# Seven-product up projection of a conv FFN: bank-freeing sum ahead of the gate's products, persistent convolution tiles, small copies on ACT, one weight and the last norms on DVE

## The chip, the cores and the metric

The kernel runs on one core of one Trainium2 chip. The core has five engines that run side by side: TensorE (PE, matrix products), VectorE (DVE, elementwise), ScalarE (ACT, elementwise functions and copies), GpSimd (POOL, elementwise) and SyncE (SP, which issues loads). PE writes into the banks of PSUM; the other operands lie in SBUF. Each engine works through its own list in order, and waits by semaphores for the others. The metric is the device time of one execution in microseconds (us).

## The reference

A decoder block on x of 1024 tokens by 1024 channels, in float32. Two token mixers are merged by gates, and a convolutional FFN follows; its part is the one that the change touches:

```
u = h @ w_up                                   # 1024 -> 2 x 2816
u = sum(up[:, i:i + T] * conv_w[i] for i in range(3)) + conv_b
gate, val = split(u, 2)
out = (gelu(gate, approximate=True) * val) @ w_down
```

The result is normalised by its root mean square over the channels, scaled, and added to the residual h.

## The kernel before

Channels lie on the 128 partitions and tokens on the free axis, in two halves of 512. A float32 product is made of three matmuls on parts: each operand is cast to a high part (`w_hi`, `b_hi`) and the rest is taken as a low part (`w_lo`, `b_lo`), and lines L225, L226 and L227 are high x high, high x low and low x high. ACT makes the casts. The subtraction of a weight's low part is made by POOL or DVE: `load_w` (L219) chooses by a count, or takes the engine named in `eng`.

The up projection has 22 pairs of channel tiles (a gate tile, index b = 0, and a value tile, b = 1). The first NSTD = 3 pairs are made by `up_std`, plainly, once per half (`hf`). Each copies a product from PSUM into `ub`, a tile with two extra columns ahead of the 512 for the three-step convolution. For the second half these two columns come from `carry`, which the first half filled: copies of 128 x 2 on POOL (L1100, L1103). The convolution `conv` is one ACT step (L1066) and two DVE steps (L1067, L1069). `gate` applies gelu on ACT (L1075 or L1223), multiplies gate and value on DVE (L1076) and stores the product to `f_d` in HBM by a DMA that ACT issues (L1077).

The other 19 pairs use seven products in place of eight (a two-by-two block scheme over halves of the channels and the halves of the tokens). Its weights are sums of weight halves, made on DVE: `w_sa` at L1175 and L1176, two more in place at L1178 and L1179. ACT casts them (L1171) and POOL subtracts (L1172), except one half that DVE does. POOL's subtraction of `w_sa` must be through before DVE may write the next `w_sa` into the same buffer two tiles later. The inputs are T1 to T4, sums of `hn2`'s halves made on DVE from `n_d`, loaded back from HBM (L1129 to L1135), with low parts at L962. The products go to the banks `ps_x`, `ps_z`, `ps_t` and `ps_y`: 84 matmuls per pair. ACT copies `ps_x` to s1 (L1197) and `ps_z` to s5 (L1205); DVE's sum L1207 reads `ps_t`, and from then on PE may run the second group into it; L1209, L1215 and L1217 are the other sums that read PSUM, and L1213 on POOL adds s1 and s5 in SBUF. For the first NEAR = 4 pairs the `ps_x` part was computed earlier and comes from HBM.

The second half of a pair's gate work (convolution of the value tile, products, stores) is the function `rest`, which the next pair's code calls, right behind the copy of s1. The order of instructions on each engine comes from a scheduler that takes the code's order and moves what has a priority (`WPRIO` for weights, `GPRIO` for `rest`).

The down projection and its norm end the kernel. `post_norm` is called for 512 tokens and then twice for 256: there each of eight output tiles is multiplied by the broadcast root `rm_b` (L931) and added to the residual (L932), shared between DVE, which reads `rm_b` from PSUM, and POOL, which reads a copy that ACT makes (L920).

## Time and profile before

| what | value |
|---|---|
| median of 3 timed runs | 1880.75 us (1874.88 to 1882.73) |
| profiled execution, its own time | 1882.48 us |
| its span, first to last instruction | 1880.7 us |
| mean granted TensorE clock | 0.978 of full speed |
| PE busy | 1788.1 us (95% of the span) |
| DVE busy | 1177.7 us (63%) |
| ACT busy | 648.9 us (35%) |
| POOL busy | 687.7 us (37%) |

Busy PE time contains overlap of pipelined matmuls, so the number of matmuls that start in a stretch tells more than its busy share. The seven-product loop fills the stretch from about 1250 to 1611 us, its steady part the stretch from 1345 to 1565; the down projection and the last norm follow to the end.

### The profile page before, as it was taken

The page shows a single profiled execution, that of the slowest core. Times are in us where ns is not written, and L with a number is a line of the kernel's source. Part 1 is how long each engine was busy: PE and PEld are TensorE (multiplying, and loading weights), DVE is VectorE, ACT ScalarE, POOL GpSimd, SP SyncE. Part 2 cuts the span into 40 slices and gives each one's busy share as a digit, 9 for nine tenths or more (in the row PEclk, how much of TensorE's full clock was granted, in tenths as well). Part 3 has the DMA queues.
Part 4 walks back from the last instruction along what each step waited for, and adds up shares of the span by engine and source line. Part 5 has one row for each costly group of instructions (what it writes and reads, how often), then busy time and mean ns, then how long its engine had stood idle before and what let it go on. Part 6 is the DMA issues. An engine that isn't in the chain of part 4 may idle for free.

```text
span 1880.7 us, 27396 instructions
## 1 busy us (share of the span) xinstructions
PE 1788.1 (95%) x10610; PEld 1450.5 (77%) x10610; DVE 1177.7 (63%) x2068; ACT 648.9 (35%) x993; POOL 687.7 (37%) x491
## 2 busy tenths in 40 slices
PE   8879999999999999999999999888999999999996
PEld 7657778788777878888788778667777777878885
DVE  4786584754667635664353746789988888753413
ACT  6543221111111113232333344544444445443320
POOL 1344522311221112101463754554545445223523
PEclk9889999999999999999999999989999999999998
DMA  8233532342333325655553744533222221775531
GB/s 291 85 114 101 181 90 71 115 112 89 110 94 105 84 67 169 185 153 183 192 173 96 235 162 134 185 129 118 84 86 72 79 90 62 223 212 148 182 93 45
DMA packets 202690, 244.44 MB, mean 130 GB/s; under 512 B 60992, under 2 KB 136256, under 8 KB 201536
## 3 DMA queue, kind: packets, MB, share of 16 engines
q1 hardware_dynamic: 125712, 171.11, 30.0%
q10 hardware_dynamic: 76848, 71.59, 11.6%
q8 instruction: 83, 1.36, 0.3%
q14 instruction: 47, 0.39, 0.1%
HBM read 177.10 MB, written 65.54 MB: 129 GB/s over the span
## 4 chain that ended last, share of the span: by engine, by line
PE 51%; DVE 20%; DMA 8%; issue 5%; POOL 3%; ACT 3%; ACTq 0%; SPq 0%; DVEq 0%; POOLq 0%
PE ps_side L225 7%; PE ps_side L226 7%; PE ps_side L227 7%; DVE u_f L1067 4%; PE ps_dn L227 3%; PE ps_dn L226 3%; PE ps_dn L225 3%; DVE u_f L1069 3%; POOL w_lo L1172 2%; PE ps_o L226 1%; PE ps_o L227 1%; PE ps_o L225 1%; DVE w_sa L1176 1%; DVE xprod L629 1%; PE ps_b L227 1%
## 5 line engine op out<-in xcount | busy, mean ns | idle before, releaser
L219 POOL TENSOR_TENSOR w_lo<-w_st,w_hi 128x1024 fp32r<-128x1024 f32 (+2 forms) x111 | 260.2, 2345 | 512.2 <-ACT w_hi L213 171.2
L213 ACT CAST w_hi<-w_st 128x1024 fp32r<-128x1024 f32 (+2 forms) x162 | 161.8, 999 | 417.4 <-PE ps_side L226 123.9
L226 PE MATMUL ps_side<-hnl,w_hi 128*128 128x512 f32 x640 | 255.7, 399 | 0.0
L225 PE MATMUL ps_side<-hnh,w_hi 128*128 128x512 f32 x640 | 255.5, 399 | 0.0
L227 PE MATMUL ps_side<-hnh,w_lo 128*128 128x512 f32 x640 | 254.5, 398 | 0.0
L225 PEld LDWEIGHTS ps_side<-hnh,w_hi 128*128 128x128 f32 x640 | 120.8, 189 | 26.7 <-issue 1.5
L226 PEld LDWEIGHTS ps_side<-hnl,w_hi 128*128 128x128 f32 x640 | 120.8, 189 | 26.4 <-issue 1.5
L227 PEld LDWEIGHTS ps_side<-hnh,w_lo 128*128 128x128 f32 x640 | 120.8, 189 | 26.3 <-issue 0.8
L219 DVE TENSOR_TENSOR w_lo<-w_st,w_hi 128x1024 fp32r<-128x1024 f32 (+1 forms) x51 | 65.2, 1279 | 84.9 <-ACT w_hi L213 52.8
L1067 DVE SCALAR_TENSOR_TENSOR u_f<-ub,vct,u_f 128x512 f32<-128x512 f32 x88 | 102.6, 1183 | 15.0 <-ACT u_f L1066 15.0
L1172 POOL TENSOR_TENSOR w_lo<-w_st,w_hi 128x512 fp32r<-128x512 f32 (+1 forms) x53 | 106.2, 2026 | 4.1 <-ACT w_hi L1171 3.0
L225 PE MATMUL ps_rw<-hnh,w_hi 128*128 128x512 f32 (+1 forms) x224 | 87.3, 390 | 13.3 <-ACT hnh L290 7.0
L1066 ACT ACTIVATE u_f<-ub,vct 128x512 f32<-128x512 f32 x76 | 59.9, 813 | 101.3 <-DVE ub L1215 93.9
L226 PE MATMUL ps_rw<-hnl,w_hi 128*128 128x512 f32 (+1 forms) x224 | 86.6, 387 | 0.4 <-DVE hnl L291 0.4
L227 PE MATMUL ps_rw<-hnh,w_lo 128*128 128x512 f32 (+1 forms) x208 | 79.8, 384 | 0.0
L227 PE MATMUL ps_b<-y_hi,w_lo 128*128 128x512 f32 x192 | 75.7, 395 | 2.9 <-DVE w_lo L219 2.1
L1069 DVE SCALAR_TENSOR_TENSOR u_f<-ub,vct,u_f 128x512 f32<-128x512 f32 x88 | 78.3, 905 | 0.2
L225 PE MATMUL ps_b<-y_hi,w_hi 128*128 128x512 f32 x192 | 75.8, 395 | 0.8 <-ACT w_hi L213 0.8
L226 PE MATMUL ps_b<-y_lo,w_hi 128*128 128x512 f32 x192 | 75.4, 393 | 0.0
L225 PE MATMUL ps_dn<-f_k,w_hi 128*128 128x512 f32 (+1 forms) x198 | 72.4, 366 | 0.0
L227 PE MATMUL ps_dn<-f_k,w_lo 128*128 128x512 f32 (+1 forms) x198 | 72.4, 366 | 0.0
L226 PE MATMUL ps_dn<-f_k,w_hi 128*128 128x512 f32 (+1 forms) x198 | 72.2, 366 | 0.0
(419 smaller groups left out, 4343.5 us busy)
## 6 DMA issues: line engine op xcount, KB each, us to landing
w_st<-in_wup_dram SPq DMA_DIRECT2D x54, 512.0 KB, 3.6
w_st<-in_wch_dram SPq DMA_DIRECT2D x52, 512.0 KB, 3.9
w_st<-in_wdn_dram SPq DMA_DIRECT2D x38, 512.0 KB, 4.0
pj_d<-ot ACTq DMA_DIRECT2D x64, 256.0 KB, 2.2
zvg<-pj_d SPq DMA_DIRECT2D x8, 1536.0 KB, 9.1
f_d<-u_f ACTq DMA_DIRECT2D x44, 256.0 KB, 2.1
L<-L_d SPq DMA_DIRECT2D x8, 1344.0 KB, 6.0
w_st<-in_wbret_dram SPq DMA_DIRECT2D x16, 512.0 KB, 3.6
```

What stands on the lines that cost most here:

```text
L213: S.copy(hi, st)
L219: eng.tensor_tensor(out=lo, in0=st, in1=hi, op=ALU.subtract)
L225: PE.matmul(ps, wh, xh, start=first and a == 0, stop=False, skip_group_check=skip)
L226: PE.matmul(ps, wh, xl, start=False, stop=False, skip_group_check=skip)
L227: PE.matmul(ps, wl, xh, start=False, stop=last and a == n - 1, skip_group_check=skip)
L629: V.tensor_tensor(out=pr_[:, :, 0:t + 1], in0=xb[:, :, 0:t + 1], in1=tb[:, 0:t + 1, t].unsqueeze(1).to_broadcast([128, 8, t + 1]), op=ALU. ...
L1066: S.activation(u, src, AF.Identity, bias=VC("cb")[:, i:i + 1], scale=VC("cw2")[:, i:i + 1])
L1067: V.scalar_tensor_tensor(out=u, in0=ub[:, 1:513], scalar=VC("cw1")[:, i:i + 1], in1=u, op0=ALU.mult, op1=ALU.add)
L1069: V.scalar_tensor_tensor(out=u, in0=ub[:, 0:512], scalar=VC("cw0")[:, i:i + 1], in1=u, op0=ALU.mult, op1=ALU.add)
L1172: eng.tensor_tensor(out=w[1][:, ks, :], in0=src, in1=w[0][:, ks, :], op=ALU.subtract)
L1176: V.tensor_tensor(out=sa[:, rh_, :], in0=st1[:, lh, :], in1=st2[:, lh, :], op=ALU.subtract)
```

## The change

`gate` no longer multiplies; it returns a function that does (product and store). `rest` returns these functions, and the loop calls them right behind the sum L1207 (L1212 in the changed kernel), with a priority. For the first four pairs `rest` is called behind the copy of s5 and no longer ahead of the loads. Four `ub` tiles are made once, their first two columns set once, and used in turn, where each pair took tiles from a pool and set them by two memsets on POOL (L1190). The copies to and from `carry` go from POOL to ACT. In the second half of `up_std`, the weights whose low part DVE makes are (0, 1) and (1, 0), where it was (0, 1) alone. The last two norms are all on DVE, and ACT's copy of `rm_b` is gone.

```diff
@@ post_norm
             rb = rms_bcast(np_, ss, nt // 128)
-            if nt < 512:
-                rs_ = np_.tile([128, 512], F32, tag="ss", name="rb_s")[:, 0:nt]
-                S.copy(rs_, rb)
...
                 if nt < 512:
-                    E, r = (G, rs_) if c in ((1, 3, 5) if t0 + nt == T else (1, 2, 4, 5, 7)) else (V, rb)
-                    E.tensor_tensor(out=prs[c], in0=prs[c], in1=r, op=ALU.mult)
-                    E.tensor_tensor(out=prs[c], in0=prs[c], in1=xt, op=ALU.add)
+                    V.tensor_tensor(out=prs[c], in0=prs[c], in1=rb, op=ALU.mult)
+                    V.tensor_tensor(out=prs[c], in0=prs[c], in1=xt, op=ALU.add)
@@ gate
-            V.tensor_tensor(out=u0, in0=u0, in1=u1, op=ALU.mult)
-            nc.scalar.dma_start(f_d[hf, j], u0)
+            def product():
+                V.tensor_tensor(out=u0, in0=u0, in1=u1, op=ALU.mult)
+                nc.scalar.dma_start(f_d[hf, j], u0)
+            return product
@@ up_std
-            ws = [load_w(wup[j + FT * b], 8, eng=V if late and b else None) for b in range(2)]
+            ws = [load_w(wup[j + FT * b], 8, eng=V if hf and (j, b) in ((0, 1), (1, 0)) else None) for b in range(2)]
...
-                    G.tensor_copy(ub[:, 0:2], carry[:, 2 * j + b, :])
+                    S.copy(ub[:, 0:2], carry[:, 2 * j + b, :])
                 S.copy(ub[:, 2:514], ps)
                 if hf == 0:
-                    G.tensor_copy(carry[:, 2 * j + b, :], ub[:, 512:514])
+                    S.copy(carry[:, 2 * j + b, :], ub[:, 512:514])
                 cv.append(conv(es, ub, b, j, ps))
-            gate(j, hf, *cv)
+            gate(j, hf, *cv)()
@@ seven-product loop
         def rest():
-            pass
+            return []
+        ubs = [[fp.tile([128, 1026], F32, name=f"ub{b}{q}", bufs=1) for b in range(2)] for q in range(2)]
+        for q in range(2):
+            for b in range(2):
+                G.memset(ubs[q][b][:, 0:2], 0.0)
...
-            ub = [fp.tile([128, 1026], F32, tag=f"ub{b}", name="ub") for b in range(2)]
-            for b in range(2):
-                G.memset(ub[b][:, 0:2], 0.0)
+            ub = ubs[n % 2]
...
                 with tc.issue_after(c1.ins), tc.high_priority(offset=GPRIO):
-                    rest()
+                    last = rest()
             else:
-                rest()
...
-            S.copy(s5, pZ)
+            c5 = S.copy(s5, pZ)
+            if n < NEAR:
+                with tc.issue_after(c5.ins), tc.high_priority(offset=GPRIO):
+                    last = rest()
             mmb(pT, w2, range(4, 8), T3, True, True)
-            V.tensor_tensor(out=s5, in0=pT, in1=s5, op=ALU.add)
+            a5 = V.tensor_tensor(out=s5, in0=pT, in1=s5, op=ALU.add)
+            with tc.issue_after(a5.ins), tc.high_priority(offset=2 * GPRIO):
+                for f in last:
+                    f()
...
             def rest(j=j, part=part, u0=u0):
-                gate(j, 0, u0[0], part(1, 0), gelu=False)
-                gate(j, 1, u0[1], part(1, 1))
-        rest()
+                return [gate(j, 0, u0[0], part(1, 0), gelu=False), gate(j, 1, u0[1], part(1, 1))]
+        for f in rest():
+            f()
```

In the changed kernel the lines have other numbers: the convolution steps L1067 and L1069 are L1063 and L1065 there, the product L1076 is L1075, its store L1077 is L1076, the sum L1207 is L1212, L1209 is L1217, L1215 is L1223, L1217 is L1225, L1213 is L1221, the weight sums L1175 and L1176 are L1179 and L1180, the casts L1171 and cuts L1172 are L1175 and L1176, and the copies L1197 and L1205 are L1199 and L1206.

On DVE, in a pair of the steady loop, these rows stand in the kernel before (the value tile's last convolution steps, the products, the sum of `ps_t`, that of `ps_y`, and the weight sums of a later pair):

```order
L1069 SCALAR_TENSOR_TENSOR u_f<-ub,vct,u_f 128x512 x2
L1076 TENSOR_TENSOR u_f<-u_f 128x512 x2
L1207 TENSOR_TENSOR s_12888<-ps_t,s_12888 128x512
L1209 TENSOR_TENSOR s_12887<-ps_y,s_12887 128x512
L1175 TENSOR_TENSOR w_sa<-w_st 128x512
L1176 TENSOR_TENSOR w_sa<-w_st 128x512
L1178 TENSOR_TENSOR w_st<-w_sa,w_st 128x512
```

And these at the same place in the changed kernel:

```order
L1065 SCALAR_TENSOR_TENSOR u_f<-ub_11019,vct,u_f 128x512 x2
L1212 TENSOR_TENSOR s_12840<-ps_t,s_12840 128x512
L1075 TENSOR_TENSOR u_f<-u_f 128x512 x2
L1217 TENSOR_TENSOR s_12839<-ps_y,s_12839 128x512
L1179 TENSOR_TENSOR w_sa<-w_st 128x512
L1180 TENSOR_TENSOR w_sa<-w_st 128x512
L1182 TENSOR_TENSOR w_st<-w_sa,w_st 128x512
```

The two products moved from ahead of the sum of `ps_t` to behind it; the rest keeps its place.

On ACT, in a pair of the steady loop, before (the gelu, the copy of s5, the stores of the products, the cast of `w_sa` that POOL's subtraction reads):

```order
L1075 ACTIVATE u_f<-u_f 128x512
L1205 COPY s_11831<-ps_z 128x512
L1077 DMA f_d<-u_f 128x512
L1171 CAST w_hi<-w_sa 128x1024
L1077 DMA f_d<-u_f 128x512
L1171 CAST w_hi<-w_st 128x512 x2
L1212 COPY ub<-ps_x 128x512
```

And in the changed kernel:

```order
L1071 ACTIVATE u_f<-u_f 128x512
L1206 COPY s_11811<-ps_z 128x512
L1175 CAST w_hi<-w_sa 128x1024
L1076 DMA f_d<-u_f 128x512 x2
L1175 CAST w_hi<-w_st 128x512 x2
L1220 COPY ub_11018<-ps_x 128x512
```

The cast of `w_sa` moved ahead of both stores.

On DVE, in the third pair of the loop (near 1295 to 1302 us before), before:

```order
L1209 TENSOR_TENSOR s_11279<-ps_y,s_11279 128x512
L1069 SCALAR_TENSOR_TENSOR u_f<-ub,vct,u_f 128x512
L1175 TENSOR_TENSOR w_sa<-w_st 128x512
L1176 TENSOR_TENSOR w_sa<-w_st 128x512
L1076 TENSOR_TENSOR u_f<-u_f 128x512
L1215 TENSOR_TENSOR ub<-ps_z,s_11279 128x512
```

And in the changed kernel:

```order
L1217 TENSOR_TENSOR s_11275<-ps_y,s_11275 128x512
L1075 TENSOR_TENSOR u_f<-u_f 128x512
L1179 TENSOR_TENSOR w_sa<-w_st 128x512
L1180 TENSOR_TENSOR w_sa<-w_st 128x512
L1075 TENSOR_TENSOR u_f<-u_f 128x512
L1223 TENSOR_TENSOR ub_11018<-ps_z,s_11275 128x512
```

The first of the two products moved ahead of both `w_sa` sums.

## Rows read from the trace of the kernel before

**Rows 1.** Busy us by stage: stretch, length, each engine's busy (instructions), clock, DMA.
```profile
1200.00:1300.00 100.00, 88.45 (x353) 70.79 (x352) 83.84 (x106) 43.84 (x68) 61.34 (x33) 0.91 0.36 119
1400.00:1500.00 100.00, 97.71 (x425) 78.54 (x424) 87.88 (x96) 45.41 (x70) 50.57 (x36) 1.00 0.24 81
1700.00:1800.00 100.00, 100.00 (x450) 83.06 (x449) 36.37 (x45) 36.46 (x50) 42.43 (x22) 1.00 0.55 167
...
1214.00:1218.00 4.00, 4.00 (x10) 3.14 (x11) 0.00 (x0) 0.00 (x0) 2.47 (x3) 0.50 0.59 147
1620.00:1660.00 40.00, 40.00 (x179) 33.10 (x178) 24.85 (x23) 18.86 (x28) 12.01 (x5) 1.00 0.67 203
```

**Rows 2.** The chain that ended last, 1345.8 to 1564.7: start, us, what.
```profile
1345.88 1.32 DVE u_f L1067 x2
...
1564.61 0.66 DVE u_f L1067
```

**Rows 3.** Waits from 1345.8 to 1564.7: us in total, times, longest.
```profile
ACT w_hi L1171 <- DVE u_f L1076: 32.4, 11, 3.0
DVE w_sa L1175 <- POOL w_lo L1172: 23.8, 11, 2.2
PE ps_t L225 <- DVE s L1207: 4.6, 10, 0.5
```

**Rows 4.** Timeline of one steady tile: start, us, engine, line; ACT, POOL, DVE.
```profile
1445.44 0.56 ACT L1205 COPY s<-ps_z 128x512 f32<-128x512 f32 x1
...
1448.97 1.05 ACT L1171 CAST w_hi<-w_sa 128x1024 fp32r<-128x1024 f32 x1 [2.96 <-DVE u_f L1076]
...
1450.09 2.40 POOL L1172 TENSOR_TENSOR w_lo<-w_sa,w_hi 128x1024 fp32r<-128x1024 f32 x1 [1.91 <-ACT w_hi L1171]
...
1452.52 1.77 DVE L1175 TENSOR_TENSOR w_sa<-w_st 128x512 f32<-128x512 f32 x1 [2.16 <-POOL w_lo L1172]
```

**Rows 5.** Waits of PE from 1200 to 1345.
```profile
PE ps_z L225 <- ACT s L1205: 5.5, 1, 5.5
PE ps_up L227 <- POOL w_lo L219: 5.2, 1, 5.2
PE ps_z L227 <- POOL ub L1190: 3.1, 1, 3.1
PE ps_z L227 <- POOL w_lo L1172: 2.7, 1, 2.7
```

**Rows 6.** Timeline of POOL at the start of the stage.
```profile
1201.46 10.14 POOL L1100 COPY ub<-carry 128x2 f32<-128x2 f32 x1 [6.03 <-DMA e_d<-e_s]
...
1214.10 2.37 POOL L219 TENSOR_TENSOR w_lo<-w_st,w_hi 128x1024 fp32r<-128x1024 f32 x1
...
1253.28 5.25 POOL L1172 TENSOR_TENSOR w_lo<-w_sa,w_hi 128x1024 fp32r<-128x1024 f32 x1 [3.58 <-ACT w_hi L1171]
```

**Rows 7.** Timeline of DVE and POOL in the tile from 1327.49 on.
```profile
1327.49 1.41 DVE L1067 SCALAR_TENSOR_TENSOR u_f<-ub,vct,u_f 128x512 f32<-128x512 f32 x2
...
1345.81 0.74 DVE L1067 SCALAR_TENSOR_TENSOR u_f<-ub,vct,u_f 128x512 f32<-128x512 f32 x1
...
1330.46 2.62 POOL L1172 TENSOR_TENSOR w_lo<-w_sa,w_hi 128x1024 fp32r<-128x1024 f32 x1
```

**Rows 8.** Timeline of ACT near 1302.
```profile
1302.43 0.62 ACT L1171 CAST w_hi<-w_st 128x512 fp32r<-128x512 f32 x1 [11.49 <-DVE w_st L1179]
```

**Rows 9.** Timeline of DVE in the last norms.
```profile
1865.62 0.65 DVE L235 TENSOR_TENSOR rs_t<-rs_t,rs_y 128x2 f32<-128x2 f32 x1
...
1868.74 0.16 DVE L235 TENSOR_TENSOR rs_t<-rs_t,rs_y 128x2 f32<-128x2 f32 x1
...
1871.20 1.75 DVE L931 TENSOR_TENSOR pr<-pr,rm_b 128x256 f32<-128x256 f32 x5 [1.59 <-ACT rb_s L920]
1872.86 3.67 DVE L932 TENSOR_TENSOR pr<-pr,h_r 128x256 f32<-128x256 f32 x5
```

**Rows 10.** ACT's instructions by line and shape, the smallest: busy us, mean ns.
```profile
L302 ACT ACTIVATION_READ_ACCUMULATOR xn<-xn 128x1 f32 x8 | 1.5, 186 | 0.0
```

## The prediction

> **What bounds the kernel now.** I read the page first, then busy time by stage, then the waits, the chain and the timelines of the two stretches where PE is not full. The profiled execution took 1882.48 us: a span of 1880.7 us and 1.8 us around it. The sum below is made against that time. It lies 1.7 us above the median of the three timed runs (1880.75), and I leave that difference alone. For this kernel 0.5% is 9.4 us, about what a measurement can tell from no change.
>
> By stage [rows 1], a full PE issues 450 matmuls in 100 us (1700 to 1800). From 1200 to 1300 it issues 353 and from 1400 to 1500 it issues 425. So there are two places to gain, and they have different causes.
>
> The first is the steady part of the seven-product loop. The chain of what ended last passes the same DVE instruction, the first convolution step L1067, at 1345.88 and at 1564.61 with eleven equal periods between them [rows 2]: 218.73 / 11 = 19.88 us per tile. A tile is 84 matmuls, and the part that is full runs them at 0.2235 us (179 in 40 us) [rows 1]; within the steady loop they follow each other by 0.2267 us, the median of 927 gaps. So PE alone needs 84 x 0.2267 = 19.04 us. It loses 0.84 us per tile, all at one point: the last group of the tile waits for the sum L1207 that frees its bank, ten times, up to 0.5 us, and restarts a little slower [rows 3]. The sum is late because DVE's own loop takes 19.88 us: DVE waits 2.2 us in each tile at L1175 for POOL's subtraction L1172, and that one is late because ACT waits 3.0 us for the product L1076 before it makes the cast that POOL reads [rows 3]. In one tile: ACT's copy of s5 at 1445.44, its cast only at 1448.97, POOL from 1450.09 to 1452.49, L1175 at 1452.52 [rows 4]. The loop closes through DVE, ACT, POOL and DVE again; PE only follows.
>
> The second place is the start of that stage. PE waits 5.5, 5.2, 3.1 and 2.7 us there [rows 5], and after such a wait it runs slowly: from 1214 to 1218, right behind the 5.2 us wait, the granted clock is 0.50, the lower of the two levels (1.2 GHz), and 10 matmuls start in 4 us [rows 1] where a full PE starts 18. The 5.2 us wait is for a subtraction on POOL that stood behind a copy of two columns. That copy took 10.14 us from 1201.46, since DVE was in an unbroken run of instructions with two SBUF operands [rows 6].
>
> **The steady loop, step by step.** The order of the changed kernel puts ACT's cast of w_sa directly behind the copy of s5, ahead of both stores. In the tile above that copy ended at 1446.00, so the cast ends at about 1447.0 instead of 1450.01, and POOL's subtraction is ready 3.0 us earlier. The two memsets that POOL had to pass first, one of them waiting for a convolution step of the same tile, are gone. On DVE the bank-freeing sum comes ahead of the products: 2 x 0.60 us earlier. What DVE then does without its wait is seen in the one tile of before in which the cast came ahead of the store: L1067 at 1327.49 and again at 1345.81, 18.32 us, with POOL's subtraction running beside the PSUM-reading sum and one product held behind it [rows 7]. The changed order holds the same instructions there with the sum one place earlier, so I take 18.3 us for the DVE loop where POOL is let in beside the sum, and 18.9 us where it is let in between the two L1069 (0.6 us of overlap lost). Both lie under PE's 19.04, so PE becomes the pace. I take 19.10, since a small wait for the copy s1 remains (0.07 us where I read the gap). Gain: 11 x (19.88 - 19.10) = 8.6 us. Bounds: 11 x 0.84 = 9.2 above. Below, POOL and DVE in strict turns: per tile 15 DVE instructions with two SBUF operands at 0.63, POOL 8.5, and three PSUM sums of 0.60 that find no POOL work beside them, 9.5 + 8.5 + 1.8 = 19.8, so 11 x 0.1 = 1 us.
>
> What a grant to POOL costs is open, and here a page speaks against the change. In the trace a POOL instruction that comes up in a gapless run of DVE instructions waits for the end of the run: 10.14 us for one copy, and 5.25 us for a subtraction that takes 2.40 undisturbed [rows 4, 6]. The Trainium skill, page "SBUF — State Buffer", section "Who interferes with whom", says that a DVE instruction with two SBUF inputs and a GpSimd instruction that reads SBUF take turns, and that whichever starts first blocks the other for the whole instruction; it says nothing of runs. By the page POOL would be let in behind the first L1069, ahead of the bank-freeing sum, the strict-turn bound of 1 us would be the nearer one, and the sum would come out at 1873. The 10.14 us and the 5.25 us disagree with that; a rival below has its own price from rows.
>
> **The start.** The weight whose subtraction PE waited for goes to DVE, where it takes 1.2 us in the run behind eight b_lo, from about 1204.3, and PE needs it at 1208.4. The 5.2 us wait goes, and with it the slow restart (10 matmuls at 0.2235 would be 2.2 us, not 4.0: 1.8): 7.0 us. But PE then meets the next two waits 7.0 us earlier, and they hang on DVE. POOL's second subtraction, 2.37 us from 1214.10 [rows 6], moves to about 1211.5; the weight load in SP's queue and the load n_d behind it, for which DVE stands idle, move by 2.6. Three DVE instructions fewer stand ahead of the first w_sa sums (3 x 0.60 = 1.8). So those waits end 4.4 us earlier, and 2.6 of the 7.0 are given back. The 5.5 us wait comes through ACT: its cast at 1302.43 sat 11.49 us on DVE's L1179 [rows 8], and the convolution step behind it then waited until the store of the product before it had landed. In the changed order the product stands ahead of two sums of w_sa that, held by POOL, took 1.77 us each as in [rows 4]: I take 3.0 us of the possible 3.5. Sum of the start: 4.4 + 3.0 = 7.4 us. Bounds: 3.0 less the 1.2 us that DVE takes on = 1.8 below; above 7.0, 3.5 and 2.9 for the subtraction of 5.25 us that would take 2.40: 13.4.
>
> **The tail.** Sixteen instructions per half go to DVE at 0.335 us each (five in 1.75) [rows 9], 5.4 us. POOL is no longer beside them, which made DVE's L932 take 3.67 us for five and the small steps of the reciprocal root 0.65 instead of 0.16 [rows 9]. First half: from 1860.3 (no copy) 5.4 + 0.35 for a sum of squares in between, then the root's chain of 2.65 as in its quiet first pass: 1868.7 against 1869.61. Second half: 1.2 us for four matmuls, then 5.4, ending at 1875.3 against 1876.54. Gain 1.2, say 1.3 with the output's issue, between -0.8 (if each takes its full 0.41: 6.6 us) and 3.
>
> **Other edits, at nothing.** Twelve two-column copies go to ACT. The nearest rows are 0.19 us (128x1) [rows 10] and 0.56 us (128x512) [rows 4], so 2.3 to 6.7 us in all, hidden under ACT's idle share: it is busy 44 of 100 us in that stage [rows 1]. I take them near the lower end, for their two columns. Uncovered, the two of a tile would cost 0.4 to 1.1 us in each of three tiles, inside the start's bounds. The four persistent tiles replace two buffers used in the same turn.
>
> **Sum.** 7.4 + 8.6 + 1.3 = 17.3 us: 1882.5 - 17.3 = **1865 us**. With all lower bounds 1.8 + 1.0 - 0.8 = 2.0 (1880), with all upper ones 13.4 + 9.2 + 3 = 25.6 (1857).
>
> **Rivals.**
> *Strict turns in the loop.* POOL gets in ahead of the bank-freeing sum in every tile and the loop stays at 19.8: 1882.5 - 7.4 - 1 - 1.3 = 1873. For it: L1175, L1176 and L1178 alternate with POOL in every steady tile. Against it: the tile of 18.32 us. Chance 0.20. By the page's rule above this would be the likeliest case.
> *The start keeps its length.* PE's first wait goes, the next ones grow by as much, since DVE, with one more subtraction, is the chain there: 1882.5 - 1.8 - 8.6 - 1.3 = 1871. For it: most of the chain there is DVE. Chance 0.17.
> *It doesn't do what it says.* Both of these at once: 1880. Chance 0.08.
> *Slower.* POOL's subtraction, ready earlier, runs ahead of the sum that frees the bank, and PE's gap at that group grows from 0.86 us to one like the start's 3.1 us wait [rows 5], behind which matmuls also ran slowly; that is the point from which it decides, since each gap then costs a slow restart of 1.8 us on top. A tile would take 20.4 (nothing beside anything: 11.9 + 8.5) + 1.8 = 22.2 us: 11 x 2.3 = 25 us lost against 8.7 won, 1899. Against it: the sum needs only PE's and ACT's results, long there, and POOL's 2.40 us alone move it to about 1451, a gap of 2.1. Chance 0.07.
>
> **Numbers.** The forecast holds 0.48 with a range of its own of 1859 to 1871. With the strict-turn and the start rivals, 1857 to 1879 leaves out some 2 in 10. Faster by over 0.5% means below 1871.3: 0.46 from the forecast, about 0.08 from each of the first two rivals, 0.62; slower 0.07; the rest, 0.31, within 0.5%.
>
> **What would show it.** Right: 19.0 to 19.2 us between the L1067 of neighbouring tiles (now L1063), no wait of DVE at w_sa, no wait of PE for the bank sum, no POOL copy of 10 us, PE's 5.2 us wait gone, L928 at 0.33 us each. Wrong: POOL's w_lo from w_sa starting between the two L1065 with the sum behind it; a period of 19.8; waits of 8 us at the first ps_z groups; ACT late with s1.

## The result, and the profile after

The changed kernel takes 1863.68 us, the median of 6 runs (1857.31 to 1865.10); the kernel before took 1880.91 us (6 runs, 1874.52 to 1882.73). The ratio is 0.991 with a 95% interval of 0.9891 to 0.9928: 17.2 us less. The profiled execution took 1864.6 us, with a span of 1862.8 us, 17.9 us less than the span before.

To see where they came from I lay the two traces side by side from one mark: PE's first matmul for the second half in `up_std`, L1088 in both kernels. Of the edits only copies of two columns lie ahead of it: the six to `carry` and, in the kernel before, the first one from it.

Timeline of PE, kernel before:

```profile
1196.19 0.50 PE L1088 MATMUL ps_up<-b_hi,w_hi 128*128 128x512 f32 x1 [1.38 <-ACT b_hi L961]
```

And of the changed kernel:

```profile
1197.99 0.50 PE L1088 MATMUL ps_up<-b_hi,w_hi 128*128 128x512 f32 x1 [1.60 <-ACT b_hi L957]
```

The part ahead of the mark came out 1.8 us longer in this execution, and no edit accounts for it (more on that at the end). A group is a run of matmuls into one bank. From the mark on, the starts of PE's groups in the two traces give four stretches, in us: the start (mark to the seventh pair's `ps_y` group), the loop (from there to the down projection's first matmul), the down projection (its first matmul to its last) and the tail (from there to the end). "Period" is the mean over ten pairs of the steady loop.

| kernel | start | loop | down | tail | mark to end | period |
|---|---|---|---|---|---|---|
| before | 165.3 | 249.7 | 248.3 | 21.2 | 684.5 | 19.88 |
| after | 157.4 | 239.3 | 248.9 | 19.2 | 664.8 | 19.04 |
| gained | 7.9 | 10.4 | -0.6 | 2.0 | 19.7 | 0.84 |

19.7 less the 1.8 at the mark are the 17.9 us of the span.

**The steady loop.** Timeline of ACT, POOL and DVE in one pair, after, to be read beside [rows 4, 7]:

```profile
1413.07 0.56 ACT L1206 COPY s<-ps_z 128x512 f32<-128x512 f32 x1
1413.54 1.05 ACT L1175 CAST w_hi<-w_sa 128x1024 fp32r<-128x1024 f32 x1
1418.18 0.93 ACTq L1076 DMA_DIRECT2D f_d<-u_f  x2
...
1396.41 2.88 POOL L1176 TENSOR_TENSOR w_lo<-w_sa,w_hi 128x1024 fp32r<-128x1024 f32 x1 [5.71 <-PE ps_y L227]
...
1414.72 2.88 POOL L1176 TENSOR_TENSOR w_lo<-w_sa,w_hi 128x1024 fp32r<-128x1024 f32 x1 [5.71 <-ACT w_hi L1175]
...
1413.95 1.40 DVE L1065 SCALAR_TENSOR_TENSOR u_f<-ub,vct,u_f 128x512 f32<-128x512 f32 x2
1415.27 0.68 DVE L1212 TENSOR_TENSOR s<-ps_t,s 128x512 f32<-128x512 f32 x1
1415.87 2.88 DVE L1075 TENSOR_TENSOR u_f<-u_f 128x512 f32<-128x512 f32 x2
1418.68 0.68 DVE L1217 TENSOR_TENSOR s<-ps_y,s 128x512 f32<-128x512 f32 x1
1419.28 0.68 DVE L1179 TENSOR_TENSOR w_sa<-w_st 128x512 f32<-128x512 f32 x1
```

The cast starts with the end of the copy of s5, and both stores stand behind it. POOL's subtraction is under way beside the bank-freeing sum L1212, the first product is held behind it (2.88 us for two products, where two undisturbed ones take 1.28, in e8 below), and the sum of `w_sa` follows with no wait. From one subtraction of POOL to the next it is 18.31 us here: DVE's own loop while it catches up. No wait of PE remains from 1345 to 1600 us, and none of DVE from 1350 to 1440. The period settles at 19.04, PE's 84 x 0.2267.

**The start.** Waits of PE from 1195 to 1345 us, after (us in total, times, longest), against [rows 5]:

```profile
PE ps_z L225 <- ACT s L1206: 4.8, 1, 4.8
PE ps_z L225 <- ACT w_hi L1175: 4.2, 2, 3.3
PE ps_z L227 <- POOL w_lo L1176: 2.4, 1, 2.4
PE ps_x L225 <- ACT s L1199: 1.7, 1, 1.7
```

Two smaller rows of the same list, PE from 1200 to 1345 us, before:

```profile
PE ps_x L225 <- ACT s L1197: 0.8, 1, 0.8
PE ps_z L225 <- ACT w_hi L1171: 0.3, 1, 0.3
```

The 5.2 us wait for POOL's w_lo and the 3.1 us wait for POOL's ub are gone, and the last of the four in time shrank from 5.5 to 4.8. Two others grew in their place: for the cast of a weight (4.2 in two, where it was 0.3) and for the copy s1 (1.7, where it was 0.8). With one more of 0.2 before and one of 0.5 after, and the wait at the mark left out, it is 17.8 us before and 13.6 after. The rest of the 7.9 us is slow running that went with the waits. Busy time by stretches of 4 us (PE, its loads, DVE, ACT, POOL, granted clock, DMA share, GB/s), after:

```profile
1214.00:1218.00 4.00, 4.00 (x19) 3.34 (x18) 1.45 (x1) 4.00 (x8) 4.00 (x2) 1.00 0.42 103
...
1250.00:1254.00 4.00, 3.39 (x7) 2.30 (x8) 3.97 (x5) 1.70 (x3) 2.97 (x5) 0.50 1.03 404
...
1306.00:1310.00 4.00, 4.00 (x19) 3.30 (x19) 4.00 (x4) 0.00 (x0) 2.77 (x3) 1.00 0.10 37
```

Where [rows 1] had 10 matmuls at the lower clock from 1214 to 1218 there are 19 at the full one; behind the second group of waits the lower clock remains; behind the 4.8 us wait, which ends at 1301.14, the full clock is back from 1306 on. In the 42 such stretches from the mark, the granted clock is short of full by 11.9 us' worth before (each stretch's 4 us times one less its clock, added up) and 6.8 us' worth after.

**The tail.** Timeline of DVE, after, against [rows 9]:

```profile
1850.61 0.16 DVE L235 TENSOR_TENSOR rs_t<-rs_t,rs_y 128x2 f32<-128x2 f32 x1
...
1853.84 2.74 DVE L927 TENSOR_TENSOR pr<-pr,rm_b 128x256 f32<-128x256 f32 x8 [1.18 <-PE rm_b L253]
1856.50 2.77 DVE L928 TENSOR_TENSOR pr<-pr,h_r 128x256 f32<-128x256 f32 x8
```

Eight L928 take 2.77 us where five took 3.67, and the root's steps take 0.16 where one of them showed 0.65. No run moves the norms alone, but the kernels below leave little else: counting before and after, the tail takes 19.2 in all eight with both norms on DVE and 21.2 in all five without.

### The profile page after: what moved, and what is told of

Its sections match the earlier page's. It is cut to its first block, busy times and chain, and to the rows that moved or that the text cites. A ratio compares the mean times of both kernels' runs of the same rounds, so it can differ in the third digit from the quotient of the medians.

```text
span 1862.8 us, 27303 instructions
## 1 busy us (share of the span) xinstructions
PE 1781.5 (96%) x10610; PEld 1450.0 (78%) x10610; DVE 1192.3 (64%) x2085; ACT 652.0 (35%) x1003; POOL 661.2 (35%) x428
## 4 chain that ended last, share of the span: by engine, by line
PE 67%; DVE 10%; DMA 8%; issue 3%; ACT 2%; POOL 1%; SPq 0%; ACTq 0%; DVEq 0%; POOLq 0%
PE ps_side L226 7%; PE ps_side L227 7%; PE ps_side L225 7%; PE ps_dn L227 3%; PE ps_dn L226 3%; PE ps_dn L225 3%; PE ps_o L226 2%; PE ps_o L227 2%; PE ps_z L225 2%; PE ps_z L227 2%; PE ps_z L226 1%; PE ps_o L225 1%; PE ps_t L225 1%; PE ps_t L226 1%; PE ps_t L227 1%
## 5 line engine op out<-in xcount | busy, mean ns | idle before, releaser
L219 DVE TENSOR_TENSOR w_lo<-w_st,w_hi 128x1024 fp32r<-128x1024 f32 (+1 forms) x52 | 67.1, 1290 | 88.1 <-ACT w_hi L213 43.4
L1176 POOL TENSOR_TENSOR w_lo<-w_st,w_hi 128x512 fp32r<-128x512 f32 (+1 forms) x53 | 104.5, 1995 | 17.2 <-PE ps_z L227 11.5
L1063 DVE SCALAR_TENSOR_TENSOR u_f<-ub,vct,u_f 128x512 f32<-128x512 f32 x88 | 91.0, 1053 | 13.2 <-ACT carry L1103 6.6
L1065 DVE SCALAR_TENSOR_TENSOR u_f<-ub,vct,u_f 128x512 f32<-128x512 f32 x88 | 96.1, 1109 | 0.2
L1176 POOL TENSOR_TENSOR w_lo<-w_sa,w_hi 128x1024 fp32r<-128x1024 f32 x19 | 52.7, 2774 | 113.0 <-ACT w_hi L1175 107.3
L1175 ACT CAST w_hi<-w_st 128x512 fp32r<-128x512 f32 (+1 forms) x72 | 49.0, 704 | 82.6 <-DVE u_f L1075 33.5
L225 PE MATMUL ps_dn<-f_k,w_hi 128*128 128x512 f32 (+1 forms) x198 | 72.4, 366 | 0.0
```

What stands on the lines that cost most here:

```text
L219: eng.tensor_tensor(out=lo, in0=st, in1=hi, op=ALU.subtract)
L225: PE.matmul(ps, wh, xh, start=first and a == 0, stop=False, skip_group_check=skip)
L1063: V.scalar_tensor_tensor(out=u, in0=ub[:, 1:513], scalar=VC("cw1")[:, i:i + 1], in1=u, op0=ALU.mult, op1=ALU.add)
L1065: V.scalar_tensor_tensor(out=u, in0=ub[:, 0:512], scalar=VC("cw0")[:, i:i + 1], in1=u, op0=ALU.mult, op1=ALU.add)
L1175: S.copy(w[0][:, ks, :], src)
L1176: eng.tensor_tensor(out=w[1][:, ks, :], in0=src, in1=w[0][:, ks, :], op=ALU.subtract)
```

## The experiments

The forecast's theory: the loop is gained by the order (cast ahead of the stores), the start by the weight on DVE, the tail by POOL's absence. The rivals: the period comes from other edits (the memsets that POOL no longer makes, the sum's place itself), or the start was gained by the copies that POOL no longer makes. For what a grant to POOL costs there are two theories: it waits for the end of a gapless run, or it takes turns with DVE instruction by instruction. Stretches of all kernels, worked out as above:

| kernel | start | loop | down | tail | mark to end | period |
|---|---|---|---|---|---|---|
| e1, order alone | 163.3 | 239.3 | 248.1 | 21.2 | 671.9 | 19.04 |
| e2, all but the order | 158.1 | 250.0 | 250.0 | 19.2 | 677.3 | 19.95 |
| e3, weight and copies alone | 157.9 | 249.4 | 250.3 | 21.2 | 678.8 | 19.88 |
| e5, copies alone | 164.2 | 249.7 | 250.1 | 21.2 | 685.2 | 19.89 |
| e6, weight alone | 157.9 | 249.6 | 247.8 | 21.2 | 676.5 | 19.89 |
| e7, memsets back | 158.9 | 239.3 | 248.6 | 19.2 | 666.0 | 19.04 |
| e8, stores alone late | 158.5 | 239.3 | 249.7 | 19.2 | 666.7 | 19.04 |
| i4, n_d loads first | 159.0 | 239.3 | 247.0 | 19.2 | 664.5 | 19.04 |
| i5, constant scalar | 157.7 | 239.3 | 249.8 | 19.2 | 666.0 | 19.04 |
| i6, i4 and i5 | 158.5 | 239.3 | 247.3 | 19.2 | 664.3 | 19.04 |
| i7, scalar from a column | 158.0 | 239.4 | 247.7 | 19.2 | 664.3 | 19.04 |

The down projection differs by up to 3.3 us between kernels in which it is the same, so differences of "mark to end" below that tell nothing.

### e1: the order alone, on the kernel before

```diff
-    V.tensor_tensor(out=u0, in0=u0, in1=u1, op=ALU.mult)
-    nc.scalar.dma_start(f_d[hf, j], u0)
+    def product(): ...
+    return product          # called behind L1212; memsets, carry, weight, norms as before
```

> The kernel before with the loop's order alone (products as functions behind the bank-freeing sum; memsets, carry copies on POOL, weights and norms as before). Theory: the steady gain comes from ACT's cast of w_sa ahead of the stores, so DVE's loop falls under PE's; period between the L1067 of neighbouring tiles 19.04 to 19.1 us instead of 19.88, about 10 us of the 17, so 1871 us, and the start's waits (5.2 us for POOL's w_lo among them) unchanged. Rival, the persistent tiles matter: POOL still passes two memsets first, one of which waits for a convolution step, the period stays at 19.5 or more and the time at 1876 or more.

Measured: 1868.61 us (5 runs), ratio 0.9939 (0.9916 to 0.9961). The period is 19.04 and the loop has its whole 10.4 us; the start keeps 163.3 (2.0 gained) and the tail 21.2. The order is enough for the loop. The start has one trace of each kernel behind it, and e5 below, which leaves PE's waits there about as they were, also shows 1.1 us less than before.

### e2: everything but the order

```diff
-            with tc.issue_after(a5.ins), tc.high_priority(offset=2 * GPRIO):
-                for f in last:
-                    f()
...
-                return [gate(j, 0, u0[0], part(1, 0), gelu=False), gate(j, 1, u0[1], part(1, 1))]
+                gate(j, 0, u0[0], part(1, 0), gelu=False)()
+                gate(j, 1, u0[1], part(1, 1))()
```

> The changed kernel with the products and stores issued at once in rest, as before; persistent tiles, ACT's carry copies, the weight on DVE and the norms on DVE kept. Theory: the period is back at 19.88 us, 8.4 us over ten periods are lost and about 1 us more in the last tiles; 1873 us. Start and tail keep their gain (8 and 2 us). Rival, the persistent tiles carry the loop: 19.04 to 19.3 us and 1864 to 1867 us.

Measured: 1870.32 us (10 runs), ratio 0.9954 (0.9935 to 0.9973). The period goes back to 19.95, and the waits of [rows 3] return. Waits from 1360 to 1570 us in e2:

```profile
ACT w_hi L1175 <- DVE u_f L1075: 32.6, 11, 3.0
DVE w_sa L1179 <- POOL w_lo L1176: 22.2, 10, 2.2
```

The cast waits 3.0 us for the product again. The start keeps its gain (158.1), and so does the tail (19.2). So the two halves of the change are nearly apart: 2.0 us of the start is the most that e1 shows of the order outside the loop, and with the weight on DVE nothing can be told, since 158.1 lies within the 157.4 to 159.0 of all kernels with that weight there. The later call of `rest` in the first four pairs goes with the order in every kernel and was not tried alone.

### e8: products ahead of the sum again, only the stores late

```diff
-            def product():
-                V.tensor_tensor(out=u0, in0=u0, in1=u1, op=ALU.mult)
+            V.tensor_tensor(out=u0, in0=u0, in1=u1, op=ALU.mult)
+            def store():
                 nc.scalar.dma_start(f_d[hf, j], u0)
...
-                S.copy(ub[0][:, 2:514], pX)
+                a5 = S.copy(ub[0][:, 2:514], pX)
+            with tc.issue_after(a5.ins), tc.high_priority(offset=2 * GPRIO):
+                for f in last:
+                    f()
```

> The changed kernel with the products back ahead of the bank-freeing sum on DVE, as before, but the stores late on ACT, behind the casts, so that the cast of w_sa waits for nothing. Theory: what counts is that the cast no longer stands behind the store; period 19.04 to 19.1 us, 1864 us as the changed kernel. Rival, the place of the sum counts: the sum comes 1.2 us later or, where POOL is let in ahead of it, up to 2.8 us later; the wait at ps_t is back and the period is 19.4 us or more, 1868 us or more.

Measured: 1860.07 us (4 runs), ratio 0.9897 (0.9873 to 0.992). Timeline of DVE and POOL in one pair of e8, where lines from the sum on are one higher than in the changed kernel:

```profile
1409.79 1.28 DVE L1074 TENSOR_TENSOR u_f<-u_f 128x512 f32<-128x512 f32 x2
1410.99 0.68 DVE L1213 TENSOR_TENSOR s<-ps_t,s 128x512 f32<-128x512 f32 x1
...
1413.36 1.76 DVE L1180 TENSOR_TENSOR w_sa<-w_st 128x512 f32<-128x512 f32 x1 [0.88 <-POOL w_lo L1177]
...
1410.04 3.30 POOL L1177 TENSOR_TENSOR w_lo<-w_sa,w_hi 128x1024 fp32r<-128x1024 f32 x1 [5.83 <-ACT w_hi L1176]
```

The products run ahead of the sum, undisturbed; POOL, ready at 1410.04, is held by them and let in beside the sum. DVE waits 0.88 us for it at `w_sa` and still keeps PE's 19.04. So it is the cast ahead of the stores that makes the loop, and the sum's place is not needed for it.

### e3, e5 and e6: what made the start

e6 is the kernel before with the weight (1, 0) on DVE, e5 the kernel before with the carry copies on ACT, and e3 has both.

```diff
-  ws = [load_w(wup[j + FT * b], 8, eng=V if late and b else None) ...                       # e3, e6
+  ws = [load_w(wup[j + FT * b], 8, eng=V if hf and (j, b) in ((0, 1), (1, 0)) else None) ...
-  G.tensor_copy(ub[:, 0:2], carry[:, 2 * j + b, :])                                         # e3, e5
+  S.copy(ub[:, 0:2], carry[:, 2 * j + b, :])
```

> The kernel before with only the carry copies on ACT and the weight (1, 0) on DVE. Theory: the 5.2 us wait of PE and its slow restart go, the first products of the loop come 7 to 8 us earlier, the loop's period stays at 19.88; 1873 us. Rival, the start keeps its length since DVE is the chain: 1 to 2 us, 1879 us.

> The kernel before with only the two-column copies on ACT. Theory: what PE waits 5.2 us for is a subtraction on POOL that comes up inside DVE's gapless run, with or without the copy ahead of it; without the copy it is held by the same run until its end and the wait stays at 4.5 to 5.2 us; gain 0 to 1.5 us. Rival, the copy's place in POOL's queue is the cause: the wait goes, 7 us from the first product of that stretch to the loop.

> The kernel before with only the low part of weight (1, 0) of the second half on DVE, copies still on POOL. Theory: the wait of 5.2 us goes, since DVE makes the subtraction inside its own run; POOL's copy is still held about 11 us and the next subtraction on POOL with it, which PE needs about 5 us later; 5 to 7.5 us of the 7.9 that the changed kernel gains there. Rival, the copy is the cause: POOL's copy still blocks, PE waits for the next subtraction instead; 0 to 2 us.

Measured: e3 1871.99 us, ratio 0.9964 (0.9948 to 0.998); e5 1878.38, 1.0004 (0.9983 to 1.0024); e6 1873.09, 0.9975 (0.9962 to 0.9989); 10 runs each. The weight alone gives the start 7.4 us in e6's trace, with the copies no more. By the timed runs e6 gains 4.7 us in all (2.1 to 7.1) and e3 6.8 (3.8 to 9.8), so the size is less sure than the trace makes it look. The copies alone give nothing that can be told, and e5 shows why. Timeline of POOL, then a wait of PE, in e5:

```profile
1200.64 12.86 POOL L219 TENSOR_TENSOR w_lo<-w_st,w_hi 128x1024 fp32r<-128x1024 f32 x1 [5.59 <-DVE b_lo L962]
```

```profile
PE ps_up L227 <- POOL w_lo L219: 5.7, 1, 5.7
```

Without the copy ahead of it, the subtraction itself comes up in the same DVE run and is held through it: 12.86 us for work of 2.40, and PE waits 5.7 us for it where it waited 5.2. In e6 the copy is still there and still held; POOL's timeline in e6:

```profile
1195.51 10.22 POOL L1100 COPY ub<-carry 128x2 f32<-128x2 f32 x3 [6.12 <-DMA e_d<-e_s]
```

The row has three copies, of which the first takes 9.97. PE no longer waits for what stands behind it. What counts here is which work sits on POOL while DVE's run lasts, not how small it is.

### e7: the memsets back in each pair

```diff
-        ubs = [[fp.tile([128, 1026], F32, name=f"ub{b}{q}", bufs=1) ...
-            ub = ubs[n % 2]
+            ub = [fp.tile([128, 1026], F32, tag=f"ub{b}", name="ub") for b in range(2)]
+            for b in range(2):
+                G.memset(ub[b][:, 0:2], 0.0)
```

> The changed kernel with tiles from the pool and two memsets per pair on POOL, as before. Theory: POOL's subtraction then starts behind the second memset, which waits for the convolution steps, and so beside the bank-freeing sum as now: period 19.04 us, start and tail as in the changed kernel. Rival: period 19.3 us or more.

Measured: 1857.18 us, one run. The period is 19.04; mark to end is 666.0 against 664.8, within what the down projection alone varies. The memsets ahead of POOL's subtraction cost nothing that shows once the cast is early.

### e9: what lets POOL in

A kernel of its own: runs of nine DVE instructions of 128x512 back to back, with one POOL instruction that becomes ready behind the third and reads its result.

```diff
+  for i, k in enumerate(ops):                  # nine
+      if k == "s": V.tensor_tensor(out=os[i], in0=x, in1=b, op=ALU.add)              # two in SBUF
+      elif k == "q": V.tensor_tensor(out=os[i], in0=x, in1=q, op=ALU.add)            # q in PSUM
+      elif k == "c": V.tensor_tensor(out=os[i], in0=os[i - 1] if i else x, in1=x, op=ALU.add)
+      elif k == "t": V.scalar_tensor_tensor(out=os[i], in0=x, scalar=a[:, 511:512], in1=b, ...)
+      if i == 2: G.tensor_copy(p[:, 0:2], os[2][:, 0:2])
```

> None of the reference's work: eight runs of nine DVE instructions of 128x512 back to back, and in each one POOL instruction that reads the third one's output. Theory (DVE keeps its turn through a gapless run of instructions with two SBUF inputs): a copy of two columns takes 3.5 us or more in a run of tensor-tensor instructions with both inputs in SBUF, 0.2 us where one input is in PSUM; with one PSUM-reading instruction as the seventh it gets in there, after about 2 us; a memset takes 0.1 us. Rival, the rule of turns by instruction: the copy never takes over 0.9 us.

The whole kernel takes 64.08 us. Timeline of POOL in e9. The copies follow in the order nine s, nine q, nine t, six s with q as seventh, six s with t as seventh, nine c; then a subtraction and a memset in nine s. From the fifth c on, DVE ran c's and the subtraction's s's in turn:

```profile
10.03 3.59 POOL L191 COPY r<-o_ss 128x2 f32<-128x2 f32 x1 [9.60 <-DVE o_ss L181]
15.60 0.18 POOL L191 COPY r<-o_qq 128x2 f32<-128x2 f32 x1 [1.98 <-DVE o_qq L183]
21.18 0.65 POOL L191 COPY r<-o_tt 128x2 f32<-128x2 f32 x1 [5.39 <-DVE o_tt L187]
26.96 1.79 POOL L191 COPY r<-o_sq 128x2 f32<-128x2 f32 x1 [5.14 <-DVE o_sq L181]
32.37 1.79 POOL L191 COPY r<-o_st 128x2 f32<-128x2 f32 x1 [3.63 <-DVE o_st L181]
38.10 0.71 POOL L191 COPY r<-o_cc 128x2 f32<-128x2 f32 x1 [3.94 <-DVE o_cc L185]
42.02 1.64 POOL L195 TENSOR_TENSOR r<-o_sw,a_in 128x512 f32<-128x512 f32 x1 [3.21 <-DVE o_sw L181]
50.29 0.10 POOL L193 MEMSET o_ms<- 128x2 f32 x1 [6.63 <-DVE o_ms L181]
```

With independent `tensor_tensor` of two SBUF operands the copy takes 3.59 us: six instructions of 0.60, the whole rest of the run. With a PSUM operand, or in a memset that reads nothing, nobody waits (0.18, 0.10). One instruction with a PSUM operand, or one `scalar_tensor_tensor` with its scalar in a column, lets the copy in after three instructions (1.79); a run of the latter, or of instructions each of which reads the one before, lets it in after one (0.65, 0.71). The subtraction got in behind one instruction too: it took 1.64, and the s behind it 1.75 instead of 0.68. So neither theory holds alone. The run of nine s blocked POOL to its end, and in the other forms it went by turns. Nor does the form settle it: in the mixed run the subtraction came in between plain `tensor_tensor` of two SBUF operands, and rows of the changed kernel near 1290 us, shown further down, have the same. What decides there stays open. The Trainium skill, page "SBUF — State Buffer", section "Who interferes with whom", has the contention of such instructions, and that a POOL instruction which only writes does not contend; 0.65 and 0.71 agree with turns and the memset's 0.10 with the second, and 3.59 and the two 1.79 do not agree with turns.

### i4 to i7: attempts on the start

In the changed kernel PE still waits there, and DVE is busy for 93% of 1200 to 1300 and 99% of 1300 to 1400. i4 lets the loads `n_d` go ahead of a weight load in SP's queue. i5 and i7 put one `scalar_tensor_tensor` into the DVE run that holds POOL, to let POOL's subtraction in; i6 is i4 and i5 together.

```diff
+                if n == 0:                                         # i4
+                    with tc.issue_after(nd2.ins):
+                        nc.sync.dma_start(st1, wup[j])
...
-            V.tensor_tensor(out=b_, in0=b_, in1=t, op=ALU.subtract)   # for c = 0, in i5 and i7
+            V.scalar_tensor_tensor(out=b_, in0=b_, scalar=1.0, in1=t, op0=ALU.mult, op1=ALU.subtract)            # i5
+            V.scalar_tensor_tensor(out=b_, in0=b_, scalar=C("ones")[:, 0:1], in1=t, op0=ALU.mult, op1=ALU.subtract)  # i7
```

> The changed kernel with the loads of n_d for the third channel tile ahead, in SP's queue, of the first weight load of the loop, which waits for a POOL subtraction that DVE's run holds (6.72 us from 1208.62). Theory: DVE's idle time from 1213 to 1219.6 shrinks by about 4 us and the loop's first waits end 2 to 4 us earlier; 663 to 661 us from the first product of the second half's up_std to the end, where the changed kernel has 664.8. Rival: the weights then come later and PE waits for w_sa as before; no change.

> The changed kernel with one instruction of DVE's long run, the first L1133, written as a scalar-tensor-tensor with the factor 1.0 (same values, 0.66 us instead of 0.60). Theory (a gapless run of tensor-tensor instructions keeps POOL out, another form lets it in): POOL's subtraction ends at about 1212 instead of 1215.3, the weight load and n_d behind it move by 3 us, and the loop's first products by 2 to 4 us; 661 to 663 us on the same measure. Rival, the form does not matter: POOL's 6.7 us stay and so does the time.

> Both at once. Theory: the two remove the same idle time of DVE in two ways, so no more than 1 us beyond the better one; 661 us on that measure. Rival: they add up, 658 us.

> The kernel i5_stt with the factor read from a column of ones in SBUF instead of the constant 1.0; the order of instructions is the same. Theory: what lets POOL in is the scalar read from SBUF, behind which the next tensor-tensor starts 0.66 and not 0.60 us later; POOL's subtraction, 6.6 us so far, takes 3.0 to 3.6 us, the weight load behind it in SP's queue is issued 3 us earlier, and DVE's run ends 2.4 us later. Since DVE is the chain there, the time does not change by more than 1 us (664 to 666 us from the first product of the second half's up_std to the end). Rival: the run holds POOL whatever the operands are, 6.6 us.

Measured: i4 1858.18 us, ratio 0.9899 (0.988 to 0.9918); i5 1860.47, 0.9907 (0.989 to 0.9924); i6 1861.45, 0.9911 (0.989 to 0.9933); i7 1860.09, 0.9898 (0.9864 to 0.9932); 4 runs each. Every interval overlaps that of the changed kernel, and from the mark they take 664.3 to 666.0 us: the gains expected of i4, i5 and i6 did not come, and i7's time came out as expected. In i4 the first `ps_y` group comes 50.4 us behind the mark instead of 46.4: the weight is now the late one, and by the steady loop most of that is made up (159.0 against 157.4). Timeline of POOL and DVE in i5, where the rewritten L1133 is L1136, as in i7:

```profile
1203.70 9.45 POOL L219 TENSOR_TENSOR w_lo<-w_st,w_hi 128x1024 fp32r<-128x1024 f32 x2 [11.80 <-PE ps_up L1088]
...
1204.38 0.68 DVE L1136 SCALAR_TENSOR_TENSOR pr<-pr,t 128x512 f32<-128x512 f32 x1
```

And in i7:

```profile
1203.62 3.83 POOL L219 TENSOR_TENSOR w_lo<-w_st,w_hi 128x1024 fp32r<-128x1024 f32 x1 [10.99 <-ACT ub L1100]
...
1205.12 2.88 DVE L1136 SCALAR_TENSOR_TENSOR pr<-pr,cst,t 128x512 f32<-128x512 f32 x1
```

With a constant for its scalar the instruction ran like its neighbours and POOL's first subtraction, held as in the changed kernel (6.72), took 6.64 us (the row has two). With the scalar from a column POOL got in ahead of it: 3.83 us, and the weight load that waits for POOL left SP 14.5 us behind the mark, not 17.4. The end did not move. What POOL took, DVE gave (2.88 us for L1136), and DVE is the full one there; that this is why is argued, not shown. No kernel tried is clear of the changed one.

## Why the prediction was right, and where it was not

**Total.** 1865 forecast, 1863.7 measured, inside the range. The terms were not all right: together they were 17.3, and 19.7 us came from the mark on, of which this execution's longer part ahead of the mark took back 1.8. That the total came out so close is in part luck: loop, start and tail together gave 3.0 us more than their terms, and the part ahead of the mark and the down projection (0.6 longer), which the change does not touch, took most of that back.

**The loop, 8.6 forecast, 10.4 measured.** The mechanism stood: cast behind the copy of s5, no wait of DVE at `w_sa`, POOL beside the bank-freeing sum, one product held, 18.3 us for DVE's loop, PE the pace. e1 and e2 show the order as its cause. Two sizes were off. The period is 19.04 and not 19.10, since no wait for s1 remained: 11 x 0.06 = 0.7, which is the upper bound of 9.2. And the stretch from the eleventh period's end to the down projection, which I left out, gave 1.2 more. I had also counted the sum's move ahead of the products and the memsets' removal as parts of it; e8 and e7, which each take one of them back, show that neither is needed by itself.

**Strict turns in the loop (0.20) and the slower case (0.07)** did not come. In the tile shown, POOL's subtraction becomes ready only 0.5 us before the bank-freeing sum, so there is little to take turns about; in e8, where it is ready 1 us before the sum with two products of SBUF operands between, it still came in beside the sum. At this place the hold of [rows 6] was the better guide.

**The start, 7.4 forecast, 7.9 measured, by two errors that cancelled.** The step "those waits end 4.4 us earlier" was mis-sized: the first `ps_y` group begins 46.4 us behind the mark, where it was 54.3, so 7.9 us. The shift of the n_d load was right. DVE's first L1129 behind it begins 2.9 us nearer to the mark than before, where I had 2.6. But from there to the sum of `w_sa` I counted three instructions fewer, 1.8 us, and it was 4.7. Timeline of DVE, before:

```profile
1220.68 2.07 DVE L1129 TENSOR_TENSOR t<-pr,t 128x512 f32<-128x512 f32 x1 [9.13 <-DMA t<-n_d]
...
1224.54 2.89 DVE L1069 SCALAR_TENSOR_TENSOR u_f<-ub,vct,u_f 128x512 f32<-128x512 f32 x1
...
1237.83 0.68 DVE L1175 TENSOR_TENSOR w_sa<-w_st 128x512 f32<-128x512 f32 x1
```

And after:

```profile
1219.59 2.07 DVE L1129 TENSOR_TENSOR t<-pr,t 128x512 f32<-128x512 f32 x2 [3.71 <-DMA t<-n_d]
...
1232.06 0.68 DVE L1179 TENSOR_TENSOR w_sa<-w_st 128x512 f32<-128x512 f32 x1
```

Before, L1129 took 2.07 and L1069 2.89 us where 0.68 and 0.74 are undisturbed, because POOL's subtractions ran at that time and held them: 1.4 + 2.2 us. After, POOL ran its three while DVE stood waiting for n_d, and the last of them held DVE for only 0.8 us (2.07 for two where 1.28 is undisturbed): 2.8 us more than the three instructions. From mark to `w_sa` it is 34.1 us instead of 41.6. That POOL's late work lengthens DVE's chain was in the trace, and I did not count it.

The step "I take 3.0 us of the possible 3.5" for the fourth wait failed: it went from 5.5 to 4.8. Timeline of DVE, POOL and ACT at that place, after:

```profile
1289.72 0.68 DVE L1075 TENSOR_TENSOR u_f<-u_f 128x512 f32<-128x512 f32 x1
1290.32 1.77 DVE L1179 TENSOR_TENSOR w_sa<-w_st 128x512 f32<-128x512 f32 x1
1292.01 1.76 DVE L1180 TENSOR_TENSOR w_sa<-w_st 128x512 f32<-128x512 f32 x1
1293.69 1.77 DVE L1075 TENSOR_TENSOR u_f<-u_f 128x512 f32<-128x512 f32 x1
...
1289.87 1.67 POOL L1221 TENSOR_TENSOR ub<-s,s 128x512 f32<-128x512 f32 x1 [1.89 <-DVE s L1217]
1291.50 3.42 POOL L1176 TENSOR_TENSOR w_lo<-w_st,w_hi 128x512 fp32r<-128x512 f32 x2
...
1290.42 5.40 ACTq L1076 DMA_DIRECT2D f_d<-u_f  x2
1295.88 0.81 ACT L1062 ACTIVATE u_f<-ub,vct 128x512 f32<-128x512 f32 x1 [8.98 <-DVE u_f L1075]
...
1299.80 0.81 ACT L1062 ACTIVATE u_f<-ub,vct 128x512 f32<-128x512 f32 x1 [1.95 <-DMA f_d<-u_f]
1300.52 0.56 ACT L1206 COPY s<-ps_z 128x512 f32<-128x512 f32 x1
```

The first product did come ahead of the two sums. But a pair has two, and the second stands behind both sums, each held by POOL as they were before. (POOL's L1221 became ready during L1075 and was let in behind it, and POOL and DVE went by turns from there, though all four rows of DVE have two SBUF operands.) ACT issues both stores in order, so it is through them at 1295.82, and its convolution step then waits 1.95 us more until a store has landed, before it can copy s5. I had followed the product that moved and not the one that the chain went through.

**The start keeps its length (0.17)** did not come, but part of it did: waits that were 0.3 and 0.8 us grew to 4.2 and 1.7. The 1.7 is for s1, which the prediction had named as a sign of being wrong. In every kernel with that weight on DVE the start takes 157.4 to 159.0 us, whatever else was changed.

**The tail, 1.3 forecast, 2.0 measured.** Steps and durations were as forecast (0.16 for the root's steps, 0.34 to 0.35 each for L927 and L928); the 0.7 us lie within my bound of 3.

**Edits at nothing.** ACT's 128x2 copies take 0.19 us each, the lower bound I had taken, and e5's ratio of 1.0004 (0.9983 to 1.0024) shows no worth of theirs alone.

## What to carry to other kernels

When a steady loop closes through three engines, look for the one instruction that waits for something its reader doesn't need (here a cast queued behind a store); moving that alone gave all that the loop could give. When a chain passes two alike instructions, follow the last of them. A POOL instruction that PE needs soon is badly placed where it becomes ready inside a long gapless run of DVE `tensor_tensor`: it can be held to the run's end, however small it is, and in e5 moving it away only handed the wait to the POOL instruction behind it.

## What was unexpected of the hardware

- A gapless run of DVE `tensor_tensor` with both operands in SBUF could hold a POOL instruction to its end: 3.59 us for a copy of two columns in e9, 12.86 us for a subtraction in e5. A `scalar_tensor_tensor` let POOL in when its scalar came from a column (1.79 in e9, 3.83 in i7) and not when it was a constant (6.64 in i5). But POOL was also let in between plain `tensor_tensor`: twice in i7 (2.54 us from 1208.32, 2.42 from 1212.46, near the undisturbed 2.40), in e9's mixed run (1.64), and by turns near 1290 in the changed kernel. What let it in there stays open, so a run of this form is not sure to hold POOL.
- The same instructions take different times from one execution to the next: the part ahead of the mark, in which the first 6000 matmuls are identical, ended between 1187.7 and 1198.0 us in the traces here; the traces lie 4.0 us apart by 166 us and 8 by 290, and the rest arises later. This spread of 10.3 us is more than half of what the change brought, which is why kernels are compared from the mark on and by ratios over several runs. Its cause was not looked for.
